# A Mamba-2 trunk on one core: the decay blocks move from VectorE's clipped subtractions to one subtraction and ScalarE's Relu and Exp

## The chip, the cores and the metric

The kernel runs on one core of a Trainium2 chip. The core's engines have an instruction stream each and meet at semaphores: TensorE (PE in the profile; PEld is its weight load), VectorE (DVE), ScalarE (ACT), GpSimd (POOL) and SyncE (SP), whose stream here only starts DMA transfers. The metric is device time in microseconds (us) of one execution; each kernel is run several times and the median counts.

## The reference, cut to what matters

Two residual layers over 256 tokens of width 2048 in float32: a Mamba-2 SSD mixer with a gated conv FFN, then a short-convolution mixer with a gated conv FFN. The change touches only the SSD mixer, and in it the decay factors:

```python
cs = cumsum(dt * a)                       # per head, within a chunk of 128 tokens
decay = exp(where(s <= l, cs[l] - cs[s], -inf))
y_diag = einsum("gls,gkls,sgkp->lgkp", cb, decay, xdt)
states = einsum("ln,kl,lkp->kpn", b, exp(cs[end] - cs), xdt)   # carried to chunk 2
y_off  = einsum("ln,kpn,kl->lkp", c, prev, exp(cs))
```

There are 64 heads of width 64 in 8 groups of 8 heads, state size 128, and 256 tokens are two chunks. The kernel does not carry a state: for each head it forms three 128x128 blocks of decays, chunk 1 on chunk 1, chunk 1 on chunk 2 (the *cross block*) and chunk 2 on chunk 2, multiplies them with the group's C·B products, and applies them to the inputs of the head by matrix products.

## The kernel before, in words

All weights are streamed from HBM once, in *units* of 256 rows by 512 columns (881 of them, 512 KB each, numbered here in the order of the stream). A unit is loaded by SyncE (L282), rounded to fp32r by ScalarE into `wh` (L302), and VectorE forms the rest `wl = raw - wh` (L303). `raw`, `wh` and `wl` have four buffers each, so the rounding of unit i+4 waits until TensorE is through with unit i. `stream` multiplies eight units with the 256 tokens (L340, L354, L355, L357) into two PSUM tiles, called the p0 and the p1 half here (`main`, three buffers in all), and then `evac` takes the tiles out.

The SSD mixer runs group by group (loop at L769). Group g makes `cb`, the C·B products (L655 to L658); four *parts* of `ssd_decay`, two heads each (L775); the input stream `xs_stream` (eight units); the transposes to tokens `xdt` (L688, L691); `ssd_y`, which applies the decays by products on TensorE (L707, L715) and adds the skip term on VectorE (L721); the gate stream `z_stream` (eight units), taken out by a copy on ScalarE (L404), two VectorE operations (L406, L645) and a Silu (L646); and `ssd_gate`: gate product (L732), Square on ScalarE (L734), two sums on VectorE (L736, L738), a token sum on TensorE (L209), a reciprocal root in small VectorE steps, and its broadcast by TensorE (L202).

`ssd_decay` needs the cumulative sums of its two heads along the free axis, the same on all partitions. SyncE loads that broadcast, `cbc`, 256 KB on chip, from `cs_d` in DRAM (L664); `cbc` is in pool `sp` with two buffers. Six `tensor_scalar` operations on VectorE (L668, L670, L672; one for each head and block) subtract or add a column and clip at zero, one Exp on ScalarE takes the whole tile (L674), and VectorE multiplies with `cb` (L676). The decay tile `m` has three buffers.

The auxiliary PSUM tiles (`aux`) have two buffers; at the beginning they also serve the last transposes of parameter rows (L164, taken out at L165).

Nothing in the text fixes where the decays stand between the casts. A scheduler inside the framework orders each engine's stream by its own estimate of times when the program is built, and the engines then run their streams strictly in that order. So a change of one helper moves instructions of all engines through the whole mixer. The loads of ScalarE's function tables (ACT_TABLE_LOAD) are in the built program wherever Exp follows Silu or Silu follows Exp.

Of the kernel before, what the change touches and what calls it, by code (L numbers as in the profile page):

```python
# [8 lines left out]
F32 = mybir.dt.float32  # L9
F32R = mybir.dt.float32r  # L10
I32 = mybir.dt.int32
AF = mybir.ActivationFunctionType
ALU = mybir.AluOpType
# [3 lines left out]
P = 128  # L17
# [22 lines left out]
def trunk_kernel(ctx, tc, a, out):  # L40
    nc = tc.nc
    mm = nc.tensor.matmul
    act = nc.scalar.activation
    tt = nc.vector.tensor_tensor
    stt = nc.vector.scalar_tensor_tensor
    ts = nc.vector.tensor_scalar
# [29 lines left out]
    def uid(s):  # L76
        n_id[0] += 1
        return f"{s}_{n_id[0]}"
# [459 lines left out]
    for _ in range(2):  # L538
# [3 lines left out]
        out=dtw, in_=s_in[:, DI + CONVD :].rearrange("(k p) h -> p k h", p=P)  # L542
    ))

    def row_bcast(src, n, tag):
# [13 lines left out]
        out=dtw, in0=dtw,  # L559
        in1=prm[i0][:, o0 : o0 + NKD].unsqueeze(2).to_broadcast([P, NKD, NH]), op=ALU.mult,  # L560
# [20 lines left out]
    for c in range(2):  # L581
        stt(
            out=v[:, c * NH : (c + 1) * NH], in0=ps[:, c * NH : (c + 1) * NH],
# [22 lines left out]
    cs = cpool.tile([P, 2, NH], F32, tag="cs", name="cs")  # L606
# [3 lines left out]
    rem = cpool.tile([P, NH], F32, tag="rem", name="rem")  # L610
# [14 lines left out]
    sp = mixer.enter_context(tc.tile_pool(name="sp", bufs=2))  # L625
# [33 lines left out]
        return cb  # L659

    def ssd_decay(g, part, cb):
        h0 = g * HPG + part * 2
        cbc = sp.tile([P, 2, 2, P], F32, tag="cbc", name=uid("cbc"))
        nc.sync.dma_start(out=cbc, in_=cs_d[:, h0 : h0 + 2, :].partition_broadcast(P))  # L664
        m = decpool.tile([P, 2, 3, P], F32, tag="decay", name=uid("decay"))
        for h in range(2):
            hi = h0 + h
            ts(out=m[:, h, 0, :], in0=cbc[:, 0, h, :], scalar1=cs[:, 0, hi : hi + 1], scalar2=0.0,  # L668
               op0=ALU.subtract, op1=ALU.min)
            ts(out=m[:, h, 1, :], in0=cbc[:, 1, h, :], scalar1=rem[:, hi : hi + 1], scalar2=0.0,  # L670
               op0=ALU.add, op1=ALU.min)
            ts(out=m[:, h, 2, :], in0=cbc[:, 1, h, :], scalar1=cs[:, 1, hi : hi + 1], scalar2=0.0,  # L672
               op0=ALU.subtract, op1=ALU.min)
        act(m, m, AF.Exp)  # L674
        mf = m.rearrange("p h j l -> p h (j l)")
        tt(  # L676
            out=mf, in0=mf,
            in1=cb.rearrange("p j l -> p (j l)").unsqueeze(1).to_broadcast([P, 2, 3 * P]),
            op=ALU.mult,
        )  # L680
        return m
# [87 lines left out]
    for g in range(NG):  # L769
        if g % 4 == 0:  # L770
            if g:
                bs = bc_stream(g, 0)
            cs_ = bc_stream(g, 1)
        cb = ssd_cb(g)
        m = [ssd_decay(g, part, cb) for part in range(4)]  # L775
        xs = xs_stream(g)
        if g == NG // 2:
            residual_stream(yhl, range(0, 16), None, None, None)
            yhl = []
        xdt = ssd_xdt(g, xs)  # L780
        ys = ssd_y(g, m, xdt, xs)
        zs = z_stream(g)
        if g == NG - 1:
            with tc.high_priority():
                yhl += ssd_gate(g, ys, zs)
        else:
            yhl += ssd_gate(g, ys, zs)
# [109 lines left out]
    for part in range(2):  # L897
        lo, hi = FPARTS[part]
# [71 lines left out]
```

## Time and profile before

| | |
|---|---|
| median of 3 runs | 2550.66 us (2550.61 to 2550.82) |
| the profiled execution's own time | 2550.66 us |
| its span | 2548.9 us |
| granted TensorE clock | 0.998 |
| from the first decay to the last product with one | 106 us to 621 us of the span |
| weights and tables read from HBM | 474.09 MB, 187 GB/s over the span |

The page's first part gives the busy time of each engine; a busy TensorE is the union of its instructions with modelled ends, so that short waits between two products can be hidden in it. The groups by line say what one instruction costs, the timeline shows instructions in order of time with the idle time before them and what ended it, and the windows give the busy time by stage.

### The profile page before, as it was taken

The numbers are of one execution on the slowest core, as the hardware profiler recorded it, in microseconds if no ns is written. First come the engines' busy times: TensorE is split into PE (matmuls) and PEld (weight loads), VectorE is DVE, ScalarE is ACT, GpSimd is POOL, SyncE is SP. The second block draws the span as 40 slices with busy tenths as digits, with TensorE's granted clock in tenths as the row PEclk, the third lists the DMA queues.
The fourth block names the chain that finished last, engine by engine and source line by source line (L and its number), as shares of the span: only waits on it lengthen the run. The fifth ranks groups of instructions, "written<-read, shape, count | busy, mean of one in ns | idle before, by whom it ended". The sixth has DMA issues, their size and how long they took to land.

```text
span 2548.9 us, 38320 instructions
## 1 busy us (share of the span) xinstructions
PE 2531.7 (99%) x15101; PEld 2227.2 (87%) x15101; DVE 1795.7 (70%) x2601; ACT 1317.4 (52%) x1622; POOL 1.1 (0%) x8
## 2 busy tenths in 40 slices
PE   9999999999999999999999999999999999999998
PEld 9999998998888888888888888888888888888886
DVE  7798875888677776557776666666677764577764
ACT  5565543566555554345554444444555553455543
POOL 0000000000000000000000000000000000000000
PEclk9999999999999999999999999999999999999999
DMA  7566655665666666666666666666666666666664
GB/s 231 173 184 197 183 177 187 195 180 176 200 182 190 190 190 190 190 187 188 189 189 190 189 185 189 190 190 190 175 190 190 190 191 194 187 190 190 190 195 143
DMA packets 255736, 478.76 MB, mean 188 GB/s; under 512 B 17667, under 2 KB 29123, under 8 KB 255427
## 3 DMA queue, kind: packets, MB, share of 16 engines
q1 hardware_dynamic: 254643, 474.13, 62.7%
q8 instruction: 118, 1.93, 0.3%
q10 hardware_dynamic: 912, 2.18, 0.2%
q14 instruction: 63, 0.52, 0.1%
HBM read 474.09 MB, written 2.16 MB: 187 GB/s over the span
## 4 chain that ended last, share of the span: by engine, by line
PE 98%; DMA 1%; DVE 1%; ACT 0%; SPq 0%; issue 0%; DVEq 0%
PE main L385 41%; PE main L387 21%; PE main L357 9%; PE main L340 8%; PE main L354 4%; PE main L355 4%; PE main L915 3%; PE main L916 3%; PE main L917 3%; PE aux L707 1%; DMA raw<-in_ssd_w_in_dram 0%; DMA cbc<-cs_d 0%; PE aux L715 0%; PE aux L571 0%; PE aux L688 0%; PE aux L202 0%
## 5 line engine op out<-in xcount | busy, mean ns | idle before, releaser
L303 DVE TENSOR_TENSOR wl<-raw,wh 128x1024 fp32r<-128x1024 f32 (+1 forms) x881 | 1075.6, 1222 | 690.6 <-ACT wh L302 686.1
L302 ACT CAST wh<-raw 128x1024 fp32r<-128x1024 f32 (+1 forms) x881 | 923.4, 1049 | 1087.9 <-PE main L385 630.0
L385 PE MATMUL main<-hl,wh 128*128 128x512 f32 x4544 | 1427.5, 395 | 0.0
L387 PEld LDWEIGHTS main<-hl,wl 128*128 128x128 f32 x4544 | 853.4, 188 | 201.0
L387 PE MATMUL main<-hl,wl 128*128 128x256 f32 x4544 | 893.6, 278 | 0.0
L385 PEld LDWEIGHTS main<-hl,wh 128*128 128x128 f32 x4544 | 691.6, 189 | 0.1
L340 PE MATMUL main<-hl,wl 128*128 128x256 f32 x1792 | 362.0, 282 | 1.3 <-DVE wl L303 1.1
L340 PEld LDWEIGHTS main<-hl,wl 128*128 128x128 f32 x1792 | 311.0, 190 | 47.7 <-issue 3.3
L357 PE MATMUL main<-hl,wh 128*128 128x512 f32 x1024 | 321.4, 397 | 0.8 <-DVE hl L233 0.8
L354 PE MATMUL main<-hl,wh 128*128 128x256 f32 x768 | 204.3, 286 | 2.5 <-DVE tp L412 1.3
L355 PE MATMUL main<-hl,wh 128*128 128x256 f32 x768 | 203.3, 285 | 0.3
L357 PEld LDWEIGHTS main<-hl,wh 128*128 128x128 f32 x1024 | 157.5, 189 | 3.2 <-DVE hl L233 1.0
L354 PEld LDWEIGHTS main<-hl,wh 128*128 128x128 f32 x768 | 147.9, 193 | 3.5 <-issue 2.1
L355 PEld LDWEIGHTS main<-hl,wh 128*128 128x128 f32 x768 | 147.9, 193 | 1.1 <-DVE hl L233 0.7
L915 PE MATMUL main<-wh,hl 128*128 128x512 f32 x352 | 137.5, 391 | 0.8 <-DVE xtok L921 0.8
L916 PE MATMUL main<-wl,hl 128*128 128x512 f32 x352 | 137.5, 391 | 0.0
L917 PE MATMUL main<-wh,hl 128*128 128x512 f32 x352 | 136.9, 389 | 0.0
L404 ACT COPY tp<-main 128x512 f32<-128x512 f32 x128 | 74.3, 580 | 30.5 <-PE main L387 29.5
L406 DVE TENSOR_TENSOR tp<-main,tp 128x512 f32<-128x512 f32 x128 | 87.8, 686 | 1.3 <-ACT tp L404 1.2
L428 DVE SCALAR_TENSOR_TENSOR tp<-tp,prm,tp 128x255 f32<-128x255 f32 x208 | 88.5, 478 | 0.0
L915 PEld LDWEIGHTS main<-wh,hl 128*128 128x128 f32 x352 | 66.1, 188 | 15.4 <-DVE xtok L921 1.2
L917 PEld LDWEIGHTS main<-wh,hl 128*128 128x128 f32 x352 | 66.1, 188 | 14.1
(138 smaller groups left out, 1209.9 us busy)
## 6 DMA issues: line engine op xcount, KB each, us to landing
raw<-in_ffn_w_up_dram SPq DMA_DIRECT2D x352, 512.0 KB, 3.7
raw<-in_ffn_w_down_dram SPq DMA_DIRECT2D x176, 512.0 KB, 3.7
raw<-in_ssd_w_in_dram SPq DMA_DIRECT2D x159, 512.0 KB, 4.5
raw<-in_sc_w_in_dram SPq DMA_DIRECT2D x96, 512.0 KB, 4.0
raw<-in_ssd_w_out_dram SPq DMA_DIRECT2D x64, 512.0 KB, 4.1
raw<-in_sc_w_out_dram SPq DMA_DIRECT2D x32, 512.0 KB, 3.7
cbc<-cs_d SPq DMA_DIRECT2D x32, 256.0 KB, 5.6
xt<-in_x_dram SPq DMA_DIRECT2D x8, 256.0 KB, 7.1
```

Of the source, the lines that this page charges most:

```text
L302: put(nc.scalar.copy(wh[:, ks, :], raw[:, ks, :]))
L303: put(tt(out=wl[:, ks, :], in0=raw[:, ks, :], in1=wh[:, ks, :].bitcast(F32), op=ALU.subtract,))
L340: put(mm(pts[t // 2][:, t % 2, 0:T], wl[:, k, t * P : (t + 1) * P], hls[i // 2][:, i % 2, 0:T], start=False, stop=(i == n - 1),))
L354: put(mm(o[:, 0:T], wh[:, k, lw], hl[:, 0:T], start=first, stop=False))
L355: put(mm(o[:, 0:T], wh[:, k, lw], hl[:, T : 2 * T], start=False, stop=False))
L357: put(mm(o, wh[:, k, lw], hl, start=first, stop=False))
L385: follow(mm(o, wh[:, k, lw], hl, start=(i == 0), stop=False))
L387: follow(mm(o[:, 0:T], wl[:, k, lw], hl[:, 0:T], start=False, stop=(i == n - 1)))
L428: stt(out=y[:, j, d:T], in0=s[:, j, 0 : T - d], scalar=pcol(wname, (width - 1 - d) * nk + k0 + j), in1=y[:, j, d:T], op0=ALU.mult, op1=ALU ...
L915: follow(mm(pt[:, c, :], hi_, wh[:, k, :], start=(i == 0), stop=False))
L916: follow(mm(pt[:, c, :], hi_, wl[:, k, :], start=False, stop=False))
L917: follow(mm(pt[:, c, :], lo_, wh[:, k, :], start=False, stop=(i == n - 1)))
```

## The change

`ssd_decay` gets one more tile, `cbd`, of 2 chunks by 2 heads by 128, in pool `sp` (two buffers). One VectorE subtraction with a broadcast operand fills it for both heads and both chunks: own column minus `cbc`, the negative of what was clipped before. ScalarE then makes the cross block of each head in one Exp straight from `cbc` with the column `rem` as bias, without the clip (in a cross block the exponent is a sum of non-positive steps); clips `cbd` in place with Relu; and takes exp(-x) of it into the two other blocks.

```diff
-        for h in range(2):
-            hi = h0 + h
-            ts(out=m[:, h, 0, :], in0=cbc[:, 0, h, :], scalar1=cs[:, 0, hi : hi + 1], scalar2=0.0,
-               op0=ALU.subtract, op1=ALU.min)
-            ts(out=m[:, h, 1, :], in0=cbc[:, 1, h, :], scalar1=rem[:, hi : hi + 1], scalar2=0.0,
-               op0=ALU.add, op1=ALU.min)
-            ts(out=m[:, h, 2, :], in0=cbc[:, 1, h, :], scalar1=cs[:, 1, hi : hi + 1], scalar2=0.0,
-               op0=ALU.subtract, op1=ALU.min)
-        act(m, m, AF.Exp)
+        cbd = sp.tile([P, 2, 2, P], F32, tag="cbd", name=uid("cbd"))
+        tt(
+            out=cbd, in0=cs[:, :, h0 : h0 + 2].unsqueeze(3).to_broadcast([P, 2, 2, P]),
+            in1=cbc, op=ALU.subtract,
+        )
+        for h in range(2):
+            act(m[:, h, 1, :], cbc[:, 1, h, :], AF.Exp, bias=rem[:, h0 + h : h0 + h + 1])
+        act(cbd, cbd, AF.Relu)
+        act(m[:, :, 0:3:2, :], cbd.rearrange("p c h l -> p h c l"), AF.Exp, scale=-1.0)
```

In the changed kernel the subtraction is L668, the Exp of the cross blocks L673, the Relu L674 and the other Exp L675; from the product with `cb` on, line numbers are one higher than before (L677 for L676, L735 for L734, and so on).

The scheduler gives another order. On ScalarE there are 36 table loads in the built program instead of 26. The handover from group 2 to group 3, before: `tp_2697` and `tp_2704` are the copies out of the two gate tiles, `z_` the Silus, `decay_2207` is part 3 of group 2 and `decay_2764` part 0 of group 3.

```order
L404 COPY tp_2704<-main_2520 128x512
L302 CAST wh_2840<-raw_2838 128x1024
L646 ACTIVATE z_2701<-z_2701 128x512
L646 ACTIVATE z_2708<-z_2708 128x512
L302 CAST wh_2870<-raw_2868 128x1024
L674 ACT_TABLE_LOAD
L674 ACTIVATE decay_2207<-decay_2207 128x768
L302 CAST wh_2900<-raw_2898 128x1024
L674 ACTIVATE decay_2764<-decay_2764 128x768
L302 CAST wh_2930<-raw_2928 128x1024
L734 ACTIVATE tp_2712<-yg_2496 128x512
```

The same place now: `decay_2196` is part 3 of group 2, `decay_2752` and `decay_2762` are parts 0 and 1 of group 3, and `L735` is the first Square of group 2.

```order
L646 ACTIVATE z_2689<-z_2689 128x512
L673 ACT_TABLE_LOAD
L673 ACTIVATE decay_2196<-cbc_2194,rem 128x128 x2
L675 ACTIVATE decay_2196<-cbd_2197 128x2x2x128
L673 ACTIVATE decay_2752<-cbc_2750,rem 128x128 x2
L675 ACTIVATE decay_2752<-cbd_2753 128x2x2x128
L646 ACT_TABLE_LOAD
L646 ACTIVATE z_2696<-z_2696 128x512
L302 CAST wh_2824<-raw_2822 128x1024
L673 ACT_TABLE_LOAD
L673 ACTIVATE decay_2762<-cbc_2760,rem 128x128 x2
L735 ACTIVATE tp_2700<-yg_2484 128x512
```

Between the copies and the next cast there is now a Silu, then a table load, two parts' Exps, a load and the second Silu; a part's Exp stands ahead of the Square, and it reads `cbc` itself.

VectorE at the first group, before: `wl_1410` and `wl_1432` are the low parts of units 30 and 31, `prm_129` frees an `aux` buffer.

```order
L668 TENSOR_SCALAR decay_1005<-cbc_1003,cs 128x128
L303 TENSOR_TENSOR wl_1410<-raw_1407,wh_1409 128x1024
L670 TENSOR_SCALAR decay_1005<-cbc_1003,rem 128x128
L672 TENSOR_SCALAR decay_1005<-cbc_1003,cs 128x128
L303 TENSOR_TENSOR wl_1432<-raw_1429,wh_1431 128x1024
L668 TENSOR_SCALAR decay_1016<-cbc_1014,cs 128x128
L165 COPY prm_129<-aux_700 128x128
```

And now (`wl_1428` is unit 31, `wl_1450` unit 32, `wl_1472` unit 33; `cbd_1581` belongs to group 1):

```order
L303 TENSOR_TENSOR wl_1428<-raw_1425,wh_1427 128x1024
L165 COPY prm_129<-aux_700 128x128
L668 TENSOR_TENSOR cbd_1015<-cs,cbc_1012 128x512
L165 COPY prm_130<-aux_705 128x128
L668 TENSOR_TENSOR cbd_1025<-cs,cbc_1022 128x512
L303 TENSOR_TENSOR wl_1450<-raw_1447,wh_1449 128x1024
L165 COPY prm_131<-aux_710 128x32
L668 TENSOR_TENSOR cbd_1581<-cs,cbc_1578 128x512
L303 TENSOR_TENSOR wl_1472<-raw_1469,wh_1471 128x1024
L658 TENSOR_TENSOR cb_990<-aux_987,mask_101 128x384
```

The low parts of units 32 and 33 and the copies that free `aux` now stand behind the subtractions of parts 2 and 3 and of the next group's part 0, each of which waits for its own `cbc`.

TensorE at the token sum of group 2 (L209), before: it stands in unit 73, nine units into what follows the gate stream.

```order
L357 MATMUL main_3109<-hl_192,wh_2960 128x512 x2
L340 MATMUL main_3109<-hl_192,wl_2961 128x256 x2
L357 MATMUL main_3109<-hl_223,wh_2990 128x512 x2
L209 MATMUL aux_2720<-ones,nacc_397_2718 128x1 x2
L340 MATMUL main_3109<-hl_223,wl_2991 128x256 x2
```

And now, in the p1 half of unit 68, the fifth unit after the gate stream:

```order
L340 MATMUL main_2790<-hl_345,wl_2825 128x256 x2
L354 MATMUL main_2791<-hl_345,wh_2824 128x256
L355 MATMUL main_2791<-hl_345,wh_2824 128x256
L354 MATMUL main_2791<-hl_345,wh_2824 128x256
L355 MATMUL main_2791<-hl_345,wh_2824 128x256
L209 MATMUL aux_2708<-ones,nacc_409_2706 128x1 x2
L340 MATMUL main_2791<-hl_345,wl_2825 128x256 x2
```

The token sum has moved forward by some four and a half units of TensorE's work.

## The prediction

> **What bounds the kernel now.** I read the page's busy times and its chain first, then the windows over the SSD mixer.
>
> ```profile
> PE 2531.7 (99%) x15101; PEld 2227.2 (87%) x15101; DVE 1795.7 (70%) x2601; ACT 1317.4 (52%) x1622; POOL 1.1 (0%) x8
> ...
> PE 98%; DMA 1%; DVE 1%; ACT 0%; SPq 0%; issue 0%; DVEq 0%
> ...
> 100.00:160.00 60.00, 59.61 (x418) 53.41 (x417) 52.19 (x115) 36.81 (x45) 0.00 (x0) 1.00 0.65 201
> 220.00:280.00 60.00, 60.00 (x443) 54.95 (x442) 53.65 (x105) 32.51 (x42) 0.00 (x0) 1.00 0.61 175
> 580.00:640.00 60.00, 59.23 (x384) 51.98 (x383) 52.65 (x101) 33.90 (x44) 0.00 (x0) 1.00 0.57 179
> ```
>
> TensorE is the bound. VectorE has 53.65 of 60 us in a full window of the mixer, but TensorE never waits for it there: of 120 us in the first and the last window TensorE lacks 0.39 + 0.77 = 1.2 us, and that is all that VectorE's relief can give back. The question is only whether the new order makes TensorE wait. How far ahead the weights are, the timeline of ScalarE shows:
>
> ```profile
> 242.52 1.05 ACT L302 CAST wh<-raw 128x1024 fp32r<-128x1024 f32 x1 [2.07 <-PE main L355]
> ...
> 245.40 1.05 ACT L302 CAST wh<-raw 128x1024 fp32r<-128x1024 f32 x1 [0.56 <-ACT tp L734]
> ...
> 248.28 1.05 ACT L302 CAST wh<-raw 128x1024 fp32r<-128x1024 f32 x1 [1.83 <-PE main L355]
> ```
>
> Casts come 2.88 us apart, TensorE's time for a unit (24 products, 0.12 us each), and ScalarE waits for TensorE in between. With four buffers a cast may be late by three units, 8.6 us, less its own 1.05 and the low part's 1.22: some 6.4 us of cover.
>
> **The change part by part.** The durations:
>
> ```profile
> L302 ACT CAST wh<-raw 128x1024 fp32r<-128x1024 f32 x879 | 922.1, 1050 | 1085.9 <-PE main L385 630.0 <-PE main L917 126.3 <-PE main L357 115.2
> ...
> L674 ACT ACTIVATE decay<-decay 128x768 f32<-128x768 f32 x32 | 27.0, 844 | 7.0 <-DVE decay L672 6.9
> L674 ACT ACT_TABLE_LOAD x11 | 14.1, 1283 | 16.0 <-DVE decay L672 16.0
> ...
> L646 ACT ACTIVATE z<-z 128x512 f32<-128x512 f32 x16 | 9.7, 627 | 4.6 <-DVE z L645 4.5
> L589 ACT ACTIVATE dt_e<-dt_e 128x128 f32<-128x128 f32 x1 | 0.3, 308 | 0.0
> ...
> L303 DVE TENSOR_TENSOR wl<-raw,wh 128x1024 fp32r<-128x1024 f32 x879 | 1074.3, 1224 | 690.6 <-ACT wh L302 686.1 <-DMA prow<-in_ssd_conv_w_dram 0.5
> L668 DVE TENSOR_SCALAR decay<-cbc,cs 128x128 f32<-128x128 f32 x64 | 18.0, 281 | 11.0 <-DMA cbc<-cs_d 6.7 <-PE aux L715 3.9
> L732 DVE TENSOR_TENSOR yg<-yg,z 128x512 f32<-128x512 f32 x16 | 10.9, 684 | 0.7 <-ACT z L646 0.6
> ...
> 129.52 1.28 ACT L674 ACT_TABLE_LOAD   x1
> 130.82 0.85 ACT L674 ACTIVATE decay<-decay 128x768 f32<-128x768 f32 x1
> 131.57 1.04 ACT L302 CAST wh<-raw 128x1024 fp32r<-128x1024 f32 x1
> 132.50 0.84 ACT L674 ACTIVATE decay<-decay 128x768 f32<-128x768 f32 x1
> ```
>
> VectorE loses 192 x 0.28 = 53.8 us and gets 32 subtractions of 128x512, nearest L732: 32 x 0.684 = 21.9, so 31.9 us less. The broadcast column is no row's form; between L668's rate (four of 128x128, 1.1 us) and L732's I take L732's. ScalarE loses 32 x 0.844 = 27.0 and gets 64 x 0.308 + 64 x 0.627 = 59.8 (the strided output at L646's rate; at L674's per element it would be 0.56), and ten more table loads, 12.8: 45.6 us more. Both lie under TensorE as sums. A successor starts some 0.09 before the end of an instruction (1.04 us of cast, next start after 0.93), so in the ledgers a cast counts 0.95, an Exp of 128x128 0.22, of 128x512 0.54, a load 1.30, a VectorE step of 128x512 0.60 and a low part 1.15.
>
> [...]
>
> What costs is a **wait that the change adds**. ScalarE now reads `cbc` in the Exp of the cross block, so a `cbc` buffer comes free only when that Exp is done; with two buffers the load of part p+2 waits for the Exp of part p, and that Exp stands in ScalarE's stream behind table loads, Silus and casts.
>
> ```profile
> L664 SPq DMA_DIRECT2D cbc<-cs_d x32: 359/367/530, 100.5 to 570.8; - x32
> ...
> DMA to landing us min/median/max: 4.4/5.6/8.4
> ...
> SPq L664 <- DVE decay L672: 33.3, 24, 3.4
> ...
> DVE decay L668 <- DMA cbc<-cs_d: 6.7, 6, 3.4
> ...
> 230.20 0.60 PE L707 MATMUL aux<-decay,xdt 128*64 128x256 f32 x4
> 230.85 0.60 PE L707 MATMUL aux<-decay,xdt 128*64 128x256 f32 x4
> ...
> 245.69 0.42 DVE L738 TENSOR_TENSOR nacc<-tp 128x256 f32<-128x256 f32 x1
> ...
> 250.13 0.50 PE L209 MATMUL aux<-ones,nacc 128*128 128x1 f32 x4
> ```
>
> A load takes 5.6 us to land. Before, VectorE alone freed `cbc` and waited for a landing 6.7 us in all. One part's products take 0.65 us, and the token sum L209 stood 4.0 us behind the end of its input (246.1 to 250.1): it could be late.
>
> *Handover from group 2 to 3*, us after T0, the start of unit 64 on TensorE. ScalarE: cast 67 to 0.95, copy 1.45, Silu 2.0, table 3.3, part 3's cross Exp 3.7. That frees the buffer: part 1's `cbc` is issued at 3.8 and lands at 9.4. (Meanwhile Exps, load, second Silu, cast 68 to 8.1, load to 9.4.) Part 1's cross Exp ends at 9.8 and frees the buffer for part 3 of group 3: issued 9.9, landed 15.5. On VectorE that subtraction stands ahead of the second gate product: subtraction to 16.1, product to 16.7. The second Square ends at 17.3. VectorE puts the low part of unit 69 (to 17.9) and one more subtraction, whose `cbc` lands at 17.5, before the sums: 18.5, 19.1, 19.5. TensorE is at L209 at 3 x 0.65 + 4 x 2.88 + 0.65 + 16 x 0.12 = 16.0. It waits **3.5 us**, and all products behind it. The handovers 3-4, 5-6 and 6-7 have the same order: 4 x 3.5 = 14.0. Casts are not what is late: cast 69 ends at 13.4, its low part at 17.9, when TensorE is still held.
>
> *Handover 1 to 2*: part 3's cross Exp ends 0.1 before T0, so `cbc` lands at 5.6 and 11.9 in turn; ScalarE waits for the first, runs two loads, cast 52 ends at 11.7, second Silu at 16.1, Square at 18.7, sums at 21.3; L209 is due at 17.5. **3.8 us**, low part 52 included. *Handover 4 to 5* has no cross Exp between gate copies and Squares: nothing.
>
> *First group and handover 0 to 1*. The rows:
>
> ```profile
> 100.49 0.88 SPq L664 DMA_DIRECT2D cbc<-cs_d  x2
> ...
> 101.97 1.05 ACT L302 CAST wh<-raw 128x1024 fp32r<-128x1024 f32 x1 [0.98 <-PE main L357]
> ...
> 106.11 0.29 DVE L668 TENSOR_SCALAR decay<-cbc,cs 128x128 f32<-128x128 f32 x1 [3.40 <-DMA cbc<-cs_d]
> ...
> 109.29 0.29 DVE L668 TENSOR_SCALAR decay<-cbc,cs 128x128 f32<-128x128 f32 x1 [1.71 <-DMA cbc<-cs_d]
> ...
> 112.94 0.28 DVE L165 COPY prm<-aux 128x128 f32<-128x128 f32 x1
> ...
> 113.28 0.24 PE L164 MATMUL aux<-ident,prow 32*128 32x32 f32 x1 [0.26 <-DVE prm L165]
> ```
>
> The first two `cbc` land at 106.0 and 109.2, as before. Cast 30 ran at 101.97; now it stands behind the first cross Exp (106.5), and cast 31 behind two loads, a Silu and the second Exp: 112.7. The parameter copy follows unit 31's low part: 114.1, not 113.2, and TensorE's transpose is due eight products earlier in its stream: lag 2.2 us. The next copies stand behind subtractions whose `cbc` land at about 117.2 and 120.7 (freed by Exps at 111.1 and 114.7), so two further `aux` waits follow; the first products with decays come 4.5 us late. Then one decay late by 0.9, unit 36's low part by 0.9 and unit 37's by 2.1 behind `cbc` landings at 138.6 and 142.8, and the token sum by 2.8. Together **11.2 us**.
>
> Sum: 14.0 + 3.8 + 11.2 = 29.0. The profiled execution took 2550.66 us (span 2548.9 and 1.8 around it), the median of the runs: 2550.66 + 29.0 = 2579.7, say **2580 us**. With the shortest landing, 4.4, each pair in a handover gives back 2.4 us: 4 x 1.1 + 1.5 + 8 = 14, 2564 us. With 7.0, halfway from the median to the longest, 2.8 more: 4 x 6.3 + 6 + 13 = 44, 2595 us. I take the median landing.
>
> **The rivals.**
>
> *Nothing is seen*, 2550 to 2553 us: 6.4 us of cover and the 4 us at L209 hide it. For it: VectorE waits for `cbc` already, and TensorE lacks only 1.2 us. Against: the sum needs two landings in turn, 11.2 us, where the cover holds for one, and L209 stands four and a half units earlier.
>
> *Only the first group pays*, 2562 us (11.2): later landings nearer 4.4 us and ScalarE a little quicker than my ledger. Against: a handover's ledger would have to be wrong by 3.5 us out of 19.5.
>
> *Each table load costs double*: the row gives 1.28 for one, and one load stands uncovered on each of five chains, before part 3's cross Exp or the second Silu, so 5 x 1.28 = 6.4 more, 2586 us. Against it: the Exp at 130.82, 1.30 after its load began. [...]
>
> *Faster*: 1.2 us of TensorE's waits go, 2549.5. It cannot reach 0.2% (5.1 us, about what a measurement of this kernel tells from no change).
>
> **How the numbers follow.** The forecast, waits at first group and handovers (2564 to 2595), 0.62; first group only 0.15; nothing 0.13; double loads 0.06; faster 0.02; longer than 2595 otherwise 0.02. The range 2557 to 2595 leaves out nothing, faster and longer, 0.17. Slower by over 0.2%: 0.85; same 0.13; faster 0.02.
>
> **What would show it.** L209 of groups 0, 1, 2, 3, 5 and 6 with a wait on L739 of 2 to 6 us; SyncE's `cbc` loads waiting for ScalarE's cross Exp in place of L672; VectorE's subtractions waiting for DMA by far more than 6.7 us; TensorE's windows over the mixer lacking some 30 us; VectorE near 1764, ScalarE near 1363 us busy. It is wrong if TensorE's windows stay full, or if its waits end with casts (ScalarE's load) rather than with L209 and `aux` copies.

## The result and the profile after

The changed kernel takes 2588.97 us, median of four runs (2587.8 to 2596.13), against 2550.74 for the kernel before: 1.0156 times, 95% interval 1.0137 to 1.0174, or 38.2 us more. The forecast was 2580 (2557 to 2595), 29.0 us more. In the profiled execution the span went from 2548.9 to 2586.7, 37.8 us more. The page's busy times, the windows over the three stages shown before, and the groups of waits:

```profile
PE 2545.5 (98%) x15101; PEld 2238.7 (87%) x15101; DVE 1779.6 (69%) x2441; ACT 1361.4 (53%) x1728; POOL 1.1 (0%) x8
...
100.00:160.00 60.00, 50.29 (x345) 44.83 (x344) 38.58 (x64) 41.10 (x62) 0.00 (x0) 0.94 0.59 163
220.00:280.00 60.00, 56.90 (x389) 51.84 (x388) 47.06 (x79) 36.62 (x52) 0.00 (x0) 0.94 0.54 159
580.00:640.00 60.00, 57.23 (x398) 52.09 (x397) 47.47 (x80) 38.88 (x55) 0.00 (x0) 0.97 0.56 165
...
PE aux L209 <- DVE nacc L739: 16.0, 6, 3.1
PE aux L164 <- DVE prm L165: 4.7, 1, 4.7
...
DVE cbd L668 <- DMA cbc<-cs_d: 49.1, 19, 4.0
...
SPq L665 <- ACT decay L673: 35.7, 25, 4.0
SPq L665 <- DVE cbd L668: 29.4, 12, 4.7
```

In a waits row the columns are the total, the number of waits and the longest. The windows lacked 0.4, 0 and 0.8 us of TensorE before; now they lack 9.7, 3.1 and 2.8. TensorE waits 16.0 us at the token sum L209, six times (none before), and 4.7 us once for the parameter copy. VectorE waits 49.1 us for `cbc`, before 6.7; SyncE's loads wait 35.7 us for the cross Exp L673, and 29.4 us for VectorE's own subtraction, which reads `cbc` too.

Two numbers do not fit waiting alone. TensorE has 13.8 us *more* busy time for the same 15101 instructions, and the windows show a granted clock (the third number from the end) of 0.94 and 0.97 where it was 1.00. One handover shows both. First the timeline of ScalarE, SyncE, VectorE and TensorE at the handover from group 2 to 3, then windows of 3.4 us across it (TensorE's busy time comes first after the length):

```profile
243.94 1.28 ACT L673 ACT_TABLE_LOAD   x1
245.23 0.70 ACT L673 ACTIVATE decay<-cbc,rem 128x128 f32<-128x128 f32 x2
...
245.96 0.36 SPq L665 DMA_DIRECT2D cbc<-cs_d  x1
...
240.84 0.68 DVE L733 TENSOR_TENSOR yg<-yg,z 128x512 f32<-128x512 f32 x1
244.43 0.69 DVE L668 TENSOR_TENSOR cbd<-cs,cbc 128x512 f32<-128x512 f32 x1 [2.90 <-DMA cbc<-cs_d]
...
251.46 0.69 DVE L668 TENSOR_TENSOR cbd<-cs,cbc 128x512 f32<-128x512 f32 x1 [3.81 <-DMA cbc<-cs_d]
252.07 0.69 DVE L733 TENSOR_TENSOR yg<-yg,z 128x512 f32<-128x512 f32 x1
252.67 1.22 DVE L303 TENSOR_TENSOR wl<-raw,wh 128x1024 fp32r<-128x1024 f32 x1
253.80 0.68 DVE L668 TENSOR_TENSOR cbd<-cs,cbc 128x512 f32<-128x512 f32 x1
254.41 0.68 DVE L737 TENSOR_TENSOR tp<-tp,tp 128x512 f32<-128x512 f32 x1
255.12 0.42 DVE L739 TENSOR_TENSOR nacc<-tp 128x256 f32<-128x256 f32 x1
...
255.69 0.56 PE L209 MATMUL aux<-ones,nacc 128*128 128x1 f32 x2 [3.10 <-DVE nacc L739]
```

```profile
248.10:251.50 3.40, 3.40 (x31) 3.40 (x30) 0.04 (x1) 2.11 (x4) 0.00 (x0) 1.00 0.72 192
251.50:254.90 3.40, 1.09 (x10) 0.89 (x8) 3.40 (x5) 2.54 (x4) 0.00 (x0) 1.00 0.27 95
254.90:258.40 3.50, 2.70 (x13) 2.73 (x14) 3.36 (x8) 1.38 (x3) 0.00 (x0) 0.51 0.73 180
258.40:261.80 3.40, 3.40 (x18) 3.40 (x18) 2.95 (x12) 0.85 (x1) 0.00 (x0) 0.51 0.83 263
261.80:265.20 3.40, 3.40 (x30) 3.40 (x30) 1.23 (x1) 1.05 (x1) 0.00 (x0) 1.00 0.55 175
```

The chain is the one forecast. Behind the first gate product (240.84) a subtraction waits 2.9 us for the landing of its `cbc` (244.43). Meanwhile ScalarE has begun a table load (243.94); behind it come the cross Exp that frees `cbc`, the load issued 0.03 us after it (245.96), the landing 5.5 us later (251.46), and behind the subtraction the second gate product, a low part, one more subtraction and both sums. L209 waits 3.1 us. What was not forecast comes after it. Having stood most of one window, TensorE runs the next two at half clock (0.51): 18 instructions in a full window instead of 30. Five such stretches follow waits of 2.8 to 4.7 us in this trace, 27.3 us in all, which costs half of that, 13.7 us. TensorE's idle time grew by 24.0 us (span less busy: 17.2 to 41.2). Together 37.7 of the 37.8 (some 0.7 us are in both, for TensorE still stands 1.4 us inside these stretches).

### The profile page after: what moved, and what is told of

It reads as the page before. It is cut to its first block, busy times and chain, and to the rows that moved or that the text cites. A ratio compares the mean times of both kernels' runs of the same rounds, so it can differ in the third digit from the quotient of the medians.

```text
span 2586.7 us, 38285 instructions
## 1 busy us (share of the span) xinstructions
PE 2545.5 (98%) x15101; PEld 2238.7 (87%) x15101; DVE 1779.6 (69%) x2441; ACT 1361.4 (53%) x1728; POOL 1.1 (0%) x8
## 4 chain that ended last, share of the span: by engine, by line
PE 94%; ACT 2%; DMA 2%; DVE 1%; issue 1%; SPq 0%; DVEq 0%; ACTq 0%
PE main L385 41%; PE main L387 20%; PE main L357 9%; PE main L340 7%; PE main L916 3%; PE main L917 3%; PE main L918 3%; PE main L355 3%; PE main L354 2%; DMA cbc<-cs_d 1%; PE aux L708 0%; ACT wh L302 0%; ACT L673 0%; DVE wl L303 0%; ACT decay L673 0%
## 5 line engine op out<-in xcount | busy, mean ns | idle before, releaser
L354 PE MATMUL main<-hl,wh 128*128 128x256 f32 x768 | 207.8, 290 | 2.5 <-DVE tp L412 1.3
L355 PE MATMUL main<-hl,wh 128*128 128x256 f32 x768 | 208.8, 290 | 0.1
L404 ACT COPY tp<-main 128x512 f32<-128x512 f32 x128 | 74.3, 580 | 32.5 <-PE main L387 29.2
```

Of the source, the lines that this page charges most:

```text
L354: put(mm(o[:, 0:T], wh[:, k, lw], hl[:, 0:T], start=first, stop=False))
L355: put(mm(o[:, 0:T], wh[:, k, lw], hl[:, T : 2 * T], start=False, stop=False))
```

## The experiments

Two theories stood against each other in the first four runs: R, that late landings of `cbc` (freed by ScalarE's Exp) stand ahead of the sums, and S, that ScalarE's added work does it. After these S was made sharper, to B: the builder that orders the streams does not count the function table loads. Each edit makes the builder order the mixer anew unless it is said otherwise. The table collects what the profiles show: us over the kernel before by the medians of the same chip; then from the profiled execution the table loads, VectorE's wait for `cbc`, the wait at L209 and at the decay products (L708, L709 or L710), TensorE's idle time over before, and the time lost to the half clock (half the length of its stretches between 90 and 700 us).

| kernel | us over before | table loads | VectorE for `cbc` | L209 | decay products | TensorE idle | lost to clock |
|---|---|---|---|---|---|---|---|
| the change | 38.2 | 36 | 49.1 | 16.0 | 0.6 | 24.0 | 13.7 |
| e1, cross Exp from cbd | 30.8 | 40 | 17.0 | 0.2 | 10.8 | 19.6 | 11.9 |
| e2, clip on VectorE | 39.7 | 42 | 48.0 | 13.2 | 0.4 | 27.8 | 6.8 |
| e3, cross block on VectorE | 28.5 | 38 | 38.7 | 5.2 | 5.7 | 18.4 | 10.2 |
| e4, only the cross Exp moved | 11.6 | 36 | 17.7 | 3.0 | 0 | 8.4 | 1.7 |
| e5, before, no tables | -0.5 | 2 | 8.9 | 0 | 0 | 0.1 | 0 |
| e6, the change, no tables | 19.1 | 2 | 44.7 | 9.0 | 0 | 14.8 | 3.4 |
| e7, e1 without tables | 8.8 | 2 | 17.7 | 0.8 | 0 | 5.2 | 3.4 |
| e8, in place, four cbc | 20.8 | 42 | 3.2 | 0 | 6.0 | 14.1 | 3.4 |
| e9, e8 without tables | 4.1 | 2 | 4.0 | 0 | 0 | 2.8 | 0 |
| e10, in place, two cbc | 11.3 | 38 | 19.9 | 2.7 | 0.5 | 9.1 | 1.7 |
| e11, sums before subtractions | 20.4 | 56 | 0.0 | 2.6 | 1.2 | 11.0 | 6.8 |
| e12, three cbc | 13.1 | 32 | 17.2 | 3.5 | 0 | 8.1 | 5.1 |

### Who frees cbc, and what ScalarE has to do

**e1**, the cross Exp reads the subtraction's result, so that VectorE alone reads `cbc`:

```diff
+    tt(out=rem, in0=rem, in1=cs[:, 1, :], op=ALU.add)
...
-            act(m[:, h, 1, :], cbc[:, 1, h, :], AF.Exp, bias=rem[:, h0 + h : h0 + h + 1])
+            act(m[:, h, 1, :], cbd[:, 1, h, :], AF.Exp, bias=rem[:, h0 + h : h0 + h + 1], scale=-1.0)
```

> The changed kernel, but the cross Exp reads cbd (the subtraction's result) with the column rem + cs1 as bias, so VectorE alone reads cbc; every engine has the same instructions as in the change, but for one small addition. Theory R (late release: the cross Exp on ScalarE frees cbc late, two landings stand ahead of the gate's sums): VectorE's waits for cbc fall from 49 us to below 15, the six waits at the token sum L209 (16.0 us) and the half-clock stretches behind them (13.7 us lost) go: 2550 to 2558 us. Theory S (ScalarE's ten more table loads and its Relu delay casts, Silu and Square, whoever frees cbc): the waits stay, 2580 to 2595 us.

It took 2581.9 us, ratio 1.0118 (1.0103 to 1.0133): in the range of S, not of R. Yet the waits did not stay, as S had it. VectorE's wait for `cbc` fell to 17.0 us and L209's to 0.2; in their place TensorE waits for decays. The groups of TensorE's waits in e1, and its timeline on ScalarE, VectorE and TensorE ahead of the wait of group 2:

```profile
PE aux L709 <- DVE decay L678: 10.8, 4, 3.1
...
246.00 1.28 ACT L674 ACT_TABLE_LOAD   x1
247.30 0.40 ACT L674 ACTIVATE decay<-cbd,rem 128x128 f32<-128x128 f32 x1
247.60 0.62 ACT L675 ACTIVATE cbd<-cbd 128x512 f32<-128x512 f32 x1
248.12 0.39 ACT L674 ACTIVATE decay<-cbd,rem 128x128 f32<-128x128 f32 x1
248.53 1.28 ACT L647 ACT_TABLE_LOAD   x1
249.82 0.63 ACT L647 ACTIVATE z<-z 128x512 f32<-128x512 f32 x1
250.47 1.28 ACT L676 ACT_TABLE_LOAD   x1
251.77 0.63 ACT L676 ACTIVATE decay<-cbd 128x512 f32<-128x512 f32 x1
...
252.43 0.96 DVE L678 TENSOR_TENSOR decay<-decay,cb 128x768 f32<-128x768 f32 x1 [5.72 <-ACT decay L676]
...
253.44 1.12 PE L709 MATMUL aux<-decay,xdt 128*64 128x256 f32 x4 [3.14 <-DVE decay L678]
```

A Silu (L647) stands between the two Exps of one part, and brings two loads for itself. From 246.00 to 252.4 ScalarE spends 3.84 us on tables, and the decay is 3.1 us late. This row of events led to theory B.

**e2**, the clip on VectorE:

```diff
-        act(cbd, cbd, AF.Relu)
+        ts(out=cbd, in0=cbd, scalar1=0.0, scalar2=None, op0=ALU.max)
```

> The changed kernel with the clip as a maximum on VectorE in place of ScalarE's Relu; ScalarE still frees cbc, and loses 20 us of work. The built order puts L209 of groups 1 to 3 later on TensorE than in the change, near its place before. Theory R: VectorE still waits 35 to 55 us for cbc; what is late at L209 depends on where the builder puts it, so in groups 2, 3, 5 and 6 the wait shrinks below 1 us each while the first group's stays near 10 us: 2555 to 2570 us. Theory S: half of ScalarE's added load is gone, half of the waits stay, 2565 to 2575 us, and VectorE's waits for cbc fall with it.

2590.8 us, 1.0161 (1.0144 to 1.0178): both expectations missed the time, though VectorE's wait for `cbc`, 48.0 us, is in R's range. ScalarE has 10 us less work (1351.4 busy) and nothing is won; the order has 42 table loads, and L209 waits 13.2 us although the builder put it later. Of this run's 38.8 us of span 4.1 are neither in TensorE's idle time nor in the half clock; TensorE's busy time holds them, and where stays open.

**e3**, the cross block's addition and clip back on VectorE:

```diff
-            act(m[:, h, 1, :], cbc[:, 1, h, :], AF.Exp, bias=rem[:, h0 + h : h0 + h + 1])
+            ts(out=m[:, h, 1, :], in0=cbc[:, 1, h, :], scalar1=rem[:, h0 + h : h0 + h + 1], scalar2=0.0,
+               op0=ALU.add, op1=ALU.min)
+            act(m[:, h, 1, :], m[:, h, 1, :], AF.Exp)
```

> The changed kernel with the cross block's addition and clip back on VectorE (64 operations of 0.28 us, 18 us) and its Exp on ScalarE from the decay tile; subtraction, Relu and the other Exp stay as in the change. VectorE alone frees cbc. Theory R: as e1, 2550 to 2558 us, VectorE's waits for cbc below 15 us. Theory S: ScalarE's work is that of the change, so 2580 to 2595 us.

2579.5 us, 1.0108 (1.0093 to 1.0123). R's forecast fell: VectorE still waits 38.7 us for `cbc` though it frees it itself (SyncE's loads wait 45.3 us for VectorE's L673). S's range begins 0.5 us above the time.

**e4**, the kernel before with the cross Exp alone moved:

```diff
-            ts(out=m[:, h, 1, :], in0=cbc[:, 1, h, :], scalar1=rem[:, hi : hi + 1], scalar2=0.0,
-               op0=ALU.add, op1=ALU.min)
+            act(m[:, h, 1, :], cbc[:, 1, h, :], AF.Exp, bias=rem[:, hi : hi + 1])
...
-        act(m, m, AF.Exp)
+        act(m[:, :, 0:3:2, :], m[:, :, 0:3:2, :], AF.Exp)
```

> The kernel before with one part of the change alone: the cross block's Exp straight from cbc on ScalarE; the two diagonal blocks keep VectorE's clipped subtractions, one Exp for both, no Relu, no cbd. Theory R: ScalarE frees cbc, so VectorE's waits for cbc rise to 30 us or more, L209 is waited for in most handovers, 2570 to 2590 us. Theory S: without Relu little is added to ScalarE, 2551 to 2562 us.

2562.7 us, 1.0046 (1.0031 to 1.0061), between the two. ScalarE reads `cbc` here too and the order has as many table loads as the change, 36; still L209 waits only 3.0 us. But SyncE's loads wait 54.1 us for VectorE's L671 and only 8.6 for ScalarE's Exp, so here it is mostly VectorE that frees the buffer last. So neither the reading of `cbc` by ScalarE nor the number of loads is enough by itself.

### Table loads, with the order held

With Relu in place of Silu ScalarE's stream holds 2 table loads in e5, e6 and e7, against 26, 36 and 40. The built streams of TensorE, VectorE and SyncE then stay row for row what they were, and ScalarE's lacks only the loads; so the builder's order does not depend on them. These three runs, and e9 further down, are the only ones in which one thing changed. Relu takes as long as Silu here: from the change to e6 ScalarE's busy time falls by 43.9 us, and 34 loads of 1.283 are 43.6.

```diff
-            act(y, y, AF.Silu)
+            act(y, y, AF.Relu)
```

and so for the two other Silus of the mixer.

> The kernel before with Relu in place of the mixer's Silus (conv, gate), a changed computation that serves only the time: ScalarE then needs one function table from the first decay on and its table loads in the mixer are gone (some 20 of 1.28 us); the streams of all engines are otherwise row for row those of before. TensorE is the bound there, so 2549 to 2551 us under every theory.

> The changed kernel with Relu in place of the mixer's Silus, a changed computation that serves only the time: no table loads between Exp and Silu, streams of all engines otherwise row for row those of the change. Theory B (the builder that orders the streams does not count table loads; in the change's order one to three of them, 1.28 us each, stand ahead of the steps that are waited for): the waits at L209 fall from 16.0 us below 4, TensorE's half-clock stretches in the handovers go, 2552 to 2564 us. Theory R (two landings of cbc in turn, each behind ScalarE's Exp): the landings stay, L209 still waits 9 us or more, 2570 to 2585 us.

> e1 (cross Exp from cbd, VectorE alone frees cbc) with Relu in place of the mixer's Silus, for the time only. Theory B: e1's waits at the decay products (10.8 us) come from table loads between its Exps and go, 2550 to 2560 us. If the cause is instead the longer chain from VectorE to ScalarE and back that every part now has, most of e1's 31.5 us stay: 2570 to 2582 us.

e5 took 2550.8 us (1.0000, 0.9990 to 1.0009): to the kernel before its loads are free. e6 took 2570.4 (1.0075, 1.0060 to 1.0090), in R's range at its lower end: the change loses 19.1 us of its 38.2 with the loads, and keeps the other half. The timeline of VectorE in e6 at the place shown above, and the groups of waits:

```profile
241.01 0.69 DVE L668 TENSOR_TENSOR cbd<-cs,cbc 128x512 f32<-128x512 f32 x1 [2.50 <-DMA cbc<-cs_d]
...
247.17 0.69 DVE L668 TENSOR_TENSOR cbd<-cs,cbc 128x512 f32<-128x512 f32 x1 [2.95 <-DMA cbc<-cs_d]
247.78 0.68 DVE L733 TENSOR_TENSOR yg<-yg,z 128x512 f32<-128x512 f32 x1
...
250.84 0.42 DVE L739 TENSOR_TENSOR nacc<-tp 128x256 f32<-128x256 f32 x1
...
PE aux L209 <- DVE nacc L739: 9.0, 5, 4.0
...
DVE cbd L668 <- DMA cbc<-cs_d: 44.7, 19, 3.5
```

The same two landings stand ahead of the product and the sums. This wait at L209 is 1.74 us instead of 3.10, about one load of 1.28 less, and no half clock follows it: one load more or less on the chain is worth 1.3 us of waiting and up to 3.4 of clock. e7 took 2560.1 (1.0033, 1.0020 to 1.0046), just above the top of B's range: e1's waits at the decay products are gone. What is left, 8.8 us, are short waits (5.2 us of idle time, more than half of it in the first group) and two half-clock stretches (3.4).

### Landings

> The change with the differences written straight into the decay tile (no cbd, clipped and exponentiated in place there), and the room used for four cbc buffers instead of two; the cross Exp still reads cbc. The built order has six more table loads than the change (42). Theory R alone: a landing no longer waits for an Exp of the handover, VectorE's waits for cbc fall from 49 us below 15, time 2552 to 2562 us. With theory B beside it (the loads cost about half, as e6 against the change showed): TensorE still waits, now for the decays or L209 behind table loads, 2565 to 2582 us.

> e8 with Relu in place of the mixer's Silus, for the time only; the other streams are row for row those of e8. If table loads and late landings are the two causes and nothing else, both are gone here: 2550 to 2556 us, no wait over 2 us between 160 and 700 us. If the longer chain of a part (VectorE to ScalarE and back) costs by itself, 2558 us or more, as e7.

> The control for e8: the same code in place, with two cbc buffers. Theory R: VectorE's waits for cbc are back above 35 us, and the time is 8 us or more above e8's: 2575 to 2592 us. If the buffers are not what matters, it is within 4 us of e8.

The edit of e8 (four buffers), of e9 (the same without tables) and of e10 (two):

```diff
-        cbc = sp.tile([P, 2, 2, P], F32, tag="cbc", name=uid("cbc"))
+        cbc = sp.tile([P, 2, 2, P], F32, tag="cbc", name=uid("cbc"), bufs=4)
...
-        cbd = sp.tile([P, 2, 2, P], F32, tag="cbd", name=uid("cbd"))
+        d = m[:, :, 0:3:2, :]
         tt(
-            out=cbd, in0=cs[:, :, h0 : h0 + 2].unsqueeze(3).to_broadcast([P, 2, 2, P]),
-            in1=cbc, op=ALU.subtract,
+            out=d, in0=cs[:, :, h0 : h0 + 2].rearrange("p c h -> p h c").unsqueeze(3).to_broadcast([P, 2, 2, P]),
+            in1=cbc.rearrange("p c h l -> p h c l"), op=ALU.subtract,
         )
...
-        act(cbd, cbd, AF.Relu)
-        act(m[:, :, 0:3:2, :], cbd.rearrange("p c h l -> p h c l"), AF.Exp, scale=-1.0)
+        act(d, d, AF.Relu)
+        act(d, d, AF.Exp, scale=-1.0)
```

e8: 2571.8 us, 1.0085 (1.0068 to 1.0102). VectorE's wait for `cbc` is gone (3.2 us), L209's too, and the time is where R and B together had it; TensorE waits for decays (6.0 us, four times) behind 42 table loads, and 3.6 us for the parameter copy and 3.3 for casts. e9: 2555.0, 1.0015 (1.0006 to 1.0024). With the table loads gone and VectorE's wait for `cbc` at 4.0 us, 4.1 us are left of 38.2, so in this order the change's instructions by themselves cost little; L209 stands up to 2.6 units later in it than in the change. e10 was to be worse than e8 and is better: 2562.3, 1.0045 (1.0030 to 1.0060), so two buffers need not hurt (SyncE's loads wait 46.9 us for VectorE's subtraction here and 18.2 for ScalarE's Exp). Its VectorE timeline at the handover from group 2 to 3:

```profile
239.10 0.69 DVE L668 TENSOR_TENSOR decay<-cs,cbc 128x512 f32<-128x512 f32 x1
239.70 0.69 DVE L733 TENSOR_TENSOR yg<-yg,z 128x512 f32<-128x512 f32 x1
...
246.64 0.69 DVE L733 TENSOR_TENSOR yg<-yg,z 128x512 f32<-128x512 f32 x1 [1.77 <-ACT z L646]
247.58 1.22 DVE L303 TENSOR_TENSOR wl<-raw,wh 128x1024 fp32r<-128x1024 f32 x1 [0.25 <-ACT wh L302]
248.72 0.68 DVE L737 TENSOR_TENSOR tp<-tp,tp 128x512 f32<-128x512 f32 x1
249.33 1.22 DVE L303 TENSOR_TENSOR wl<-raw,wh 128x1024 fp32r<-128x1024 f32 x1
250.46 0.42 DVE L739 TENSOR_TENSOR nacc<-tp 128x256 f32<-128x256 f32 x1
```

From the first gate product on no subtraction stands ahead of the last sum, in the change there are four. That makes R sharper: not who frees the buffer, but whether a landing stands ahead of the sums on VectorE. It is not shown by e10 alone, for L209 has moved as well (the table below).

**e11** was to hold just that, by marking the subtraction and the last sum to keep the order of the program:

```diff
-        tt(
+        pin(tt(
             out=cbd, in0=cs[:, :, h0 : h0 + 2].unsqueeze(3).to_broadcast([P, 2, 2, P]),
...
-        tt(out=one, in0=sqs[0][:, 0, :], in1=sqs[0][:, 1, :], op=ALU.add)
+        pin(tt(out=one, in0=sqs[0][:, 0, :], in1=sqs[0][:, 1, :], op=ALU.add))
```

> The change with the order on VectorE held in one respect: the subtractions of group g+1 stand behind the gate's last sum of group g, so no landing of cbc stands ahead of a sum. The built order has 56 table loads (36 in the change) and L209 stands later, about where the kernel before has it. Theory R: L209's waits fall from 16.0 us below 3; the decays start later, so the products with decays may wait instead, 2555 to 2575 us. Theory B: twenty more table loads keep the time at 2575 us or more.

2571.4 us, 1.0079 (1.0064 to 1.0094). L209's waits fell from 16.0 to 2.6 us and VectorE's wait for `cbc` to nothing, as R had it, and the time is below B's 2575 us with twenty table loads more than in the change. But the builder also put L209 later, so its waits tell little of the landings (the table below). What is left is 11.0 us of idle time, 4.7 of them at the first group's parameter copy, and 6.8 of clock; how much of it the table loads bring is not shown.

**e12** adds one buffer and leaves the order near to that of the change:

```diff
-        cbc = sp.tile([P, 2, 2, P], F32, tag="cbc", name=uid("cbc"))
+        cbc = sp.tile([P, 2, 2, P], F32, tag="cbc", name=uid("cbc"), bufs=3)
...
-        one = small.tile([P, T], F32, tag="nacc1", name=uid("nacc1"))
+        one = small.tile([P, T], F32, tag="nacc1", name=uid("nacc1"), bufs=1)
```

> The change with three cbc buffers in place of two (room for it from a small tile, nacc1, that gets one buffer in place of two; that alone moves no instruction). The built order is near that of the change: L209 stands within half a unit of its place there in groups 0 to 2, 32 table loads in place of 36. Theory R (the load of a part waits for the Exp of the part two before it): one more load is under way, VectorE's waits for cbc fall from 49 us to 25 or less, L209's from 16.0 us to 8 or less, the half-clock stretches behind them go in part: 2558 to 2574 us. If the second ring (cbd, two buffers, freed by the last Exp of a part) or the table loads hold the sums as well, L209's waits stay above 10 us and the time above 2575 us.

2563.8 us, 1.0052 (1.0035 to 1.0068): the groups of waits in its trace,

```profile
PE aux L209 <- DVE nacc L739: 3.5, 5, 2.1
...
DVE cbd L668 <- DMA cbc<-cs_d: 17.2, 7, 2.9
```

are R's numbers (8 or less, 25 or less), and 25 of the 38 us come back with cbd's ring still at two. At the handover from group 2 to 3 one landing is waited for instead of two; the second subtraction now waits for the Exp that frees `cbd`:

```profile
239.36 0.69 DVE L668 TENSOR_TENSOR cbd<-cs,cbc 128x512 f32<-128x512 f32 x1 [2.21 <-DMA cbc<-cs_d]
...
242.56 0.69 DVE L668 TENSOR_TENSOR cbd<-cs,cbc 128x512 f32<-128x512 f32 x1 [1.37 <-ACT decay L675]
```

But four table loads are gone too, and L209 has moved. A wait at L209 is the time by which the sums end after TensorE gets there, and a new order moves both. The table gives both for four handovers, in us after TensorE's first product behind the gate stream (the T0 of the prediction): end of the sums / L209 due.

| kernel | 2-3 | 3-4 | 5-6 | 6-7 |
|---|---|---|---|---|
| before | 25.3 / 29.4 | 25.3 / 28.7 | 18.6 / 21.6 | 18.1 / 19.0 |
| the change | 20.2 / 17.2 | 20.0 / 17.2 | 20.1 / 17.2 | 19.7 / 17.1 |
| e6, the change, no tables | 18.8 / 17.2 | 17.9 / 17.2 | 18.3 / 17.2 | 18.1 / 17.1 |
| e10, in place, two cbc | 18.9 / 17.8 | 18.6 / 19.1 | 18.6 / 19.1 | 18.6 / 19.1 |
| e11, sums before subtractions | 29.7 / 33.5 | 29.7 / 32.5 | 17.4 / 18.2 | 20.8 / 19.2 |
| e12, three cbc | 18.3 / 18.0 | 20.0 / 19.7 | 18.3 / 18.0 | 19.8 / 19.7 |

In the first two handovers the sums end some 5 us *earlier* in the change than before; TensorE waits because L209 is due 12 us earlier. In e6, where the order is held, the sums come 1.4 to 2.1 us earlier still: that is the table loads. In e12 they come 1.9 and 1.8 us earlier in 2-3 and 5-6, with three loads on the way as in the change, and L209 is due 0.8 later. In 3-4 and 6-7 they come no earlier, and only L209's place, 2.5 us later, ends the wait. In e11 the sums of 2-3 and 3-4 come over 9 us later than in the change, and L209 15 to 16. So much of what e10, e11 and e12 win at L209 is its place on TensorE, and no run parts that from the landings.

The first group keeps its loss in all of these: for the parameter copy (L164) TensorE waits 3.6 us in e8, 4.5 in e10, 4.7 in e11 and 3.8 in e12 (4.7 in the change), and half clock behind it costs 3.4, 1.7, 3.4 and 3.4 more. In e10 and e12 that is over half of what is left.

No version beats the kernel before; it lacked 1.2 us of TensorE's time in the first and last windows of the mixer, so there was little to win.

## Why the prediction was right, and where its sum was off

The direction, the range and the place were right: TensorE waits at the handovers, at L209, for VectorE's sums, which stand behind two landings of `cbc`. By its steps:

- **Handovers 2-3, 3-4, 5-6, 6-7**: 3.5 us each; measured 3.10, 2.93, 3.09 and 2.77, 11.9 us against 14.0. The first of them: the sums were forecast at 19.5 us and L209 due at 16.0; it was 20.2 and 17.2, both somewhat late, so that the difference nearly held.
- **Handover 1-2**: 3.8 us; 1.44 measured. **Handover 4-5**: nothing, and nothing there.
- **First group and handover 0-1**: 11.2 us; TensorE lacks 9.7 us between 90 and 160, before 0.4. Three `aux` waits were to make the first products with decays 4.5 us late; it came as one of 4.7 at the parameter copy and one of 0.3. Then a late decay 0.6 (0.9 forecast), low parts 0.3 and 1.2 (0.9 and 2.1), the token sum 2.7 (2.8).
- **The sum of the waits**, 29.0: idle time grew by 24.0. **The term that was missing** is the clock, 13.7 us; without it the sum would have been 5 us too high instead of 9 too low. The prediction took every wait at its length, and in this trace waits of 2.8 to 4.7 us have half clock behind them. The time is inside the range with the clock or without it (2574.7 by the waits alone), but that it is only 9 us from 2580 comes of two errors of opposite sign.
- **VectorE** near 1764 us: 1779.6. The sum took the removed operations at 0.28 us each; back to back they start 0.20 apart (106.71, 106.91, 107.10 in the trace of before), so six take 1.28 us rather than 1.68, and 32 x (1.28 - 0.69) = 19 us go; measured 16.1. **ScalarE** near 1363: 1361.4, with the 36 loads foreseen.
- **The cause within the chain** was told too simply. The ledger has the table loads among its steps, but names the late release by ScalarE as what costs. ScalarE holds SyncE's loads for 35.7 us, VectorE's own subtraction for 29.4. With the order held, the loads alone carry half (38.2 to 19.1, e6). The other half is argued, not shown: e12, with one more buffer, gives back two thirds, but with four loads fewer and L209 due up to 2.6 us later. A wait is the small difference of a chain of 20 us and 17 us of cover, so each of several steps can be "the cause", the place that the builder gives L209 among them, and their shares need not add to the whole.
- **The rivals**: that nothing is seen, that only the first group pays, and that the kernel gets faster fell with the six waits. A doubled price of table loads is not borne out: the Exp at 245.23 starts 1.29 us after its load began, against 1.30 at 130.82 before.

What stays open: how the half that is not table loads divides between the landings and L209's place, and why e1, e2 and e3, each rebuilt, stay at 28 to 40 us. Their traces name the waits, and e7 shows that table loads carry most of e1's; for e2 and e3 no run takes one step away with the order held.

## What to carry to other kernels

When an edit lets a second engine read a double-buffered tile, look at what stands behind the reload on the in-order engines, not only at who frees the buffer: here a reduction that TensorE needs stood behind two such reloads. When a scheduler orders the streams, count what it does not see, here a load of 1.28 us that comes with every change between Exp and Silu, and look at where it has put the consumer: here L209 was due up to 12 us earlier than before, while its input came only 5 us earlier, and at 5-6 and 6-7 later. And price a wait of the bounding engine by its length plus what the clock does after it: here 13.7 us of half clock came on top of 24.0 us of idle time.

## What the runs showed of the hardware

The half clock had not been expected. Between 90 and 700 us it comes in stretches of 3.41 or 6.83 us, at 0.50, and in each trace they start whole multiples of 3.41 us apart: in the changed kernel at 114.99, 254.94, 312.96, 558.72 and 613.33. I cut the traces of the change and of the ten experiments that have such stretches into the windows of 3.41 us that this gives. All 23 windows at full clock in which TensorE was busy 41% or less were followed by half clock in the next; of 17 with 47 to 55% five were; above that none. In the changed kernel's window at 555.3 TensorE was busy for 1.31 us of the 3.41, and the next was at 0.50. After one or two windows the clock was at 1.00 again. So a wait of 3 us costs 3, 4.7 or 6.4 us by where it falls, estimated from these stretches (nothing, half of 3.41 or half of 6.83 on top): in the change 2.7 us at 153 cost no clock, 2.8 us at 613 one window and 3.1 us at 256 two. This may be why the changed kernel's runs spread by 8 us and those before by 0.2: the slowest of them, 2596.13 us, has a mean granted clock of 0.991, the others 0.993 and 0.994. It was not tried.
